# A convolution's running sum in PSUM: the taps of a centred depthwise convolution accumulated in one two-bank PSUM tile, with four PSUM banks left for the stage's products

## The chip, the core and the metric

The kernel runs on one core of a Trainium2 chip. Five engines work side by side, each through its own instructions in a fixed order: TensorE (PE in the profile, with its weight loads as PEld), VectorE (DVE), ScalarE (ACT), GpSimd (POOL) and SyncE (SP), which issues most of the DMA. ScalarE issues DMA too. The metric is the time of the whole launch on the device in microseconds (us), as a median of several runs.

## What is computed

One layer of a hybrid encoder block, over 1024 tokens and 1024 features. The part that matters here is the input projection's slice `xBC` (3072 channels), which goes through a convolution of five taps along the tokens, a bias and SiLU:

```
proj = h @ w_in[l]
q, k, v, xBC, z, dt_raw, gates = jnp.split(proj, offsets, axis=-1)
...
def depthwise_conv_centred(u, w, bias):
    pad = (w.shape[0] - 1) // 2
    out = lax.conv_general_dilated(u, w[:, None, :].astype(u.dtype), window_strides=(1,),
                                   padding=[(pad, pad)], dimension_numbers=("NWC", "WIO", "NWC"),
                                   feature_group_count=u.shape[-1])
    return out + bias

def ssd_mixer(xBC, z, dt_raw, conv_w, conv_b, A_log, dt_bias, ssd_D, ssd_norm_w):
    xBC = jax.nn.silu(depthwise_conv_centred(xBC, conv_w, conv_b))
    ...
```

After it come attention, a scan over the convolved channels, the merge of both branches and a two-layer MLP.

## The kernel before, in words

The stage that changes runs from about 415 to 716 us of the span. It makes 26 blocks of 128 channels by 1024 tokens, two blocks at a time ("a pair", 13 pairs: 12 for the convolution and one for gate channels, which is last). Matrices are float32; each operand is split into a high half (rounded, by ScalarE: CAST) and a low half (the rest, a subtraction: TENSOR_TENSOR at L154, on VectorE or on GpSimd), and a product takes three matmuls for each of four slices: high by high, high by low, low by high. So a product is 12 matmuls of 512 columns (`product`, L763 to L769), into one PSUM bank, tile `psc`.

A pair is a 2 by 2 block scheme with seven products in place of eight. `load_pair` fetches the pair's weights as two tiles, `r0` (blocks a11 and a21) and `r1` (a12 and a22), the latter with one buffer, so that the next pair's `r1` can only be fetched once this pair's last reader is done with it. GpSimd forms four sums of blocks (`ws`: sm1 to sm4). The operands `wop` of a11, a12 and a22 get their low halves from VectorE, those of sm1 to sm4 from GpSimd. The products are, in order: a11 (copied out by ScalarE as `c1`), a12 and sm2 (added by VectorE into the halves of the pair's first block, tile `pad`, called pa here), sm3 and a22 (into the second block, pb), sm1 (copied out by ScalarE as `p5`, then added by GpSimd to the right halves of pb and pa) and sm4 (added by VectorE into pa).

When a block is complete, `conv` runs: ScalarE writes tap 0 and the bias (L711), VectorE adds four more taps with four SCALAR_TENSOR_TENSOR of 128 by 1024 (L713), each reading `pad` and the accumulator `cacc` and writing `cacc`, all in SBUF, and ScalarE applies SiLU in place (L715). TensorE then transposes the result in eight pieces (`to_tokens`, tile `pst`, L730), ScalarE copies that out and stores it. `cacc` has three buffers.

The order of instructions on each engine is set at build time by a scheduler with its own estimates; the code's order is a wish. Waits are semaphores that it places. What is released in PSUM or SBUF goes to the next user of that buffer.

Of the kernel before, what the change touches and what calls it, by code (L numbers as in the profile page):

```python
# [9 lines left out]
F32 = mybir.dt.float32  # L10
F32R = mybir.dt.float32r
BF16 = mybir.dt.bfloat16
AF = mybir.ActivationFunctionType
ALU = mybir.AluOpType
# [4 lines left out]
P = 128  # L19
S = 1024  # L20
# [70 lines left out]
def block(ctx: ExitStack, tc: tile.TileContext, ia, out, upto=99, dbg=None):  # L91
    nc = tc.nc
    V, A, G, T = nc.vector, nc.scalar, nc.gpsimd, nc.tensor
# [43 lines left out]
    cwT = cp.tile([P, 120], F32, name="cwT")  # L137
    vecT = cp.tile([P, 104], F32, name="vecT")
    CB0, N1, N2, SN, BA = 0, 24, 32, 40, 56
# [117 lines left out]
    with tc.tile_pool(name="p0", bufs=1) as p0, tc.tile_pool(name="ps0", bufs=1, space=PSUM) as ps0:  # L257
# [4 lines left out]
        ps = ps0.tile([P, 512], F32, name="psv", tag="psv", bufs=2)  # L262
# [54 lines left out]
        def mod1(sl, between=None):  # L317
            g = mod_acc(p0, sl, bufs=7)
            n = 0
            try:  # L320
                while True:
                    next(g)
                    n += 1
                    if between:
                        between(n)
            except StopIteration as e:
                return e.value
# [5 lines left out]
        with tc.manual_schedule(engines={mybir.EngineType.SP, mybir.EngineType.DVE}):  # L333
# [11 lines left out]
            scale = mod1(1, first_half)  # L345
# [14 lines left out]
        ps = ps0.tile([P, 512], F32, name="psv", tag="psv", bufs=2)  # L360
# [342 lines left out]
    with tc.tile_pool(name="p2", bufs=1, reuse_waits="tile") as p2, \  # L703
            tc.tile_pool(name="ps2", bufs=1, space=PSUM, reuse_waits="tile") as ps2:

        def acc_tile():
            return p2.tile([P, S], F32, name="cacc", tag="cacc", bufs=CACC)

        def conv(i, pad):
            acc = accs.pop() if accs else acc_tile()  # L710
            A.activation(acc, pad[:, 0:S], AF.Identity, scale=cwT[:, i:i + 1], bias=vecT[:, CB0 + i:CB0 + i + 1])  # L711
            for k in range(1, 5):
                V.scalar_tensor_tensor(out=acc, in0=pad[:, k:k + S], scalar=cwT[:, 24 * k + i:24 * k + i + 1],  # L713
                                       in1=acc, op0=ALU.mult, op1=ALU.add)
            A.activation(acc, acc, AF.Silu)  # L715
            if i >= 20:
                adma(bc_d[i - 20][:, 1], acc)
                return
            if i >= 16:
                adma(bc_d[i - 16][:, 0], acc)  # L720
            late.append(lambda: to_tokens(i, acc))
# [3 lines left out]
        def to_tokens(i, y):  # L725
            st = p2.tile([P, NT, P], F32, name="cst", tag="cst", bufs=2)
            for hf in range(2):
                pt = ps2.tile([P, 512], F32, name="pst", tag="pst", bufs=2)
                for c in range(4):
                    T.transpose(pt[:, c * P:(c + 1) * P], y[:, (hf * 4 + c) * P:(hf * 4 + c + 1) * P], ident)  # L730
                A.copy(st[:, hf * 4:hf * 4 + 4], pt.rearrange("p (c n) -> p c n", c=4))
            if i >= 16:
                adma(xb_d[i - 16][:, :, 512:640], st)
            else:
                adma(xb_d[i // 4][:, :, (i % 4) * P:(i % 4 + 1) * P], st)
# [16 lines left out]
        def done(kind, i, pad):  # L752
            if kind == "conv":
                conv(i, pad)
            else:
                adma(gt_d[i], pad[:, 2:S + 2])
# [4 lines left out]
            return t  # L761

        def product(w, b):  # L763
            ps = ps2.tile([P, 512], F32, name="psc", tag="psc", bufs=6)
            for j in range(HK):
                T.matmul(ps, w[0][:, j], b[j][0], start=j == 0, stop=False)
                T.matmul(ps, w[0][:, j], b[j][1], start=False, stop=False)
                T.matmul(ps, w[1][:, j], b[j][0], start=False, stop=j == HK - 1)
            return ps  # L769
# [7 lines left out]
        H0, H1 = slice(2, 514), slice(514, 1026)  # L777
        nxt = load_pair(0)

        accs = []  # L780
        tus = [p2.tile([P, 2, 512], F32, name="u1", tag="cst", bufs=2)]
        pre = {"ws": [p2.tile([P, HK, P], F32, name="ws", tag="ws", bufs=4)],
               "c1": [p2.tile([P, 512], F32, name="c1", tag="c1", bufs=2)],
# [16 lines left out]
        for p, (kind, i0, _) in enumerate(pairs):  # L800
# [4 lines left out]
            def fifth():  # L805
                t = p2_tile("p5", [P, 512], 1)
                A.copy(t, product(w1_op(sm1, e_lo=G), H12))
                return t

            sm1 = w_sum(a21, a22, ALU.add)  # L810
            if p == LAST:
                p5 = fifth()
                for j in range(HK):
                    for q in range(2):
                        dma(H12[j][q].bitcast(F32), h12_d[q][j])
            c1 = p2_tile("c1", [P, 512], 2)
            A.copy(c1, product(w1_op(a11), H11))
            sm2 = w_sum(sm1, a11, ALU.subtract)
            tt(V, pa[:, H0], c1, product(w1_op(a12), H21), ALU.add)
            tt(V, pa[:, H1], c1, product(w1_op(sm2, e_lo=G), U2), ALU.add)  # L820
            if p == 0:
# [430 lines left out]
    with tc.tile_pool(name="p5", bufs=1, reuse_waits="tile") as p5, \  # L1252
# [41 lines left out]
        for n, (i, second) in enumerate(jobs):  # L1294
# [12 lines left out]
            for half in range(2):  # L1307
                ps = part[i][half] if i in part else ps5.tile([P, 512], F32, name="psg", tag="psg", bufs=6)
# [39 lines left out]
    with tc.tile_pool(name="p6", bufs=1, reuse_waits="tile") as p6:  # L1348
# [9 lines left out]
        def turned(hf, k):  # L1358
            ps = ps7.tile([P, 512], F32, name="pst", tag="ps1", bufs=4)
            for j in range(4):  # L1360
                T.transpose(ps[:, j * P:(j + 1) * P], x1[hf * 4 + j][:, k * P:(k + 1) * P], ident)
            return ps
# [4 lines left out]
        for t in range(NT):  # L1367
# [3 lines left out]
            for n in range(2):  # L1371
# [3 lines left out]
                ps = ps7.tile([P, 512], F32, name="pso", tag="ps2", bufs=4)  # L1375
# [12 lines left out]
            if t == 4:  # L1388
                for k in range(KT):
                    ps = turned(0, k)  # L1390
# [268 lines left out]
    with tc.tile_pool(name="p8", bufs=1, reuse_waits="tile") as p8:  # L1659
        acc = {}  # L1660
# [134 lines left out]
```

## Time and profile before

| | before |
|---|---|
| median of three runs | 2547.74 us (2547.34 to 2552.68) |
| profiled execution: its time, its span | 2555.1 us, 2553.3 us |
| TensorE busy over the span | 2422.2 us (95%) |
| VectorE, ScalarE, GpSimd busy over the span | 1779.8, 1121.7, 908.8 us |
| the pairs between 437 and 700 us: TensorE, VectorE, ScalarE, GpSimd busy | 244.83, 229.09, 127.24, 184.49 of 263.00 us |

Busy times say how full an engine is, not what holds the others up; that is read from the waits in each stretch. The profiled execution took 7.4 us more than the median of the three timed runs, and all durations here are of the profiled one.

### The profile page before, as it was taken

The page shows a single profiled execution, that of the slowest core. Times are in us where ns is not written, and L with a number is a line of the kernel's source. Part 1 is how long each engine was busy: PE and PEld are TensorE (multiplying, and loading weights), DVE is VectorE, ACT ScalarE, POOL GpSimd, SP SyncE. Part 2 cuts the span into 40 slices and gives each one's busy share as a digit, 9 for nine tenths or more (in the row PEclk, how much of TensorE's full clock was granted, in tenths as well). Part 3 has the DMA queues.
Part 4 walks back from the last instruction along what each step waited for, and adds up shares of the span by engine and source line. Part 5 has one row for each costly group of instructions (what it writes and reads, how often), then busy time and mean ns, then how long its engine had stood idle before and what let it go on. Part 6 is the DMA issues. An engine that isn't in the chain of part 4 may idle for free. (4 is left out here: it accounts for less than half of the span.)

```text
span 2553.3 us, 32339 instructions
## 1 busy us (share of the span) xinstructions
PE 2422.2 (95%) x11403; PEld 1935.0 (76%) x11403; DVE 1779.8 (70%) x2199; ACT 1121.7 (44%) x1944; POOL 908.8 (36%) x672
## 2 busy tenths in 40 slices
PE   5999999999989999999899999999898999999999
PEld 5898777777767777777667767777686888888887
DVE  5756346898866666666577787636659888667794
ACT  5455513444546666666333344343333222264430
POOL 2310107677711111110346665514107875113200
PEclk9899999999999999999999999999998999999999
DMA  7653751233541212111666675466424645464522
GB/s 262 181 164 124 231 182 62 78 96 92 165 141 58 87 54 88 55 54 50 201 194 206 190 218 164 146 197 207 152 79 140 201 151 171 177 207 132 161 84 89
DMA packets 282162, 363.38 MB, mean 142 GB/s; under 512 B 33673, under 2 KB 166513, under 8 KB 282001
## 3 DMA queue, kind: packets, MB, share of 16 engines
q1 hardware_dynamic: 209841, 285.22, 35.7%
q10 hardware_dynamic: 72160, 76.11, 8.9%
q8 instruction: 90, 1.47, 0.2%
q14 instruction: 71, 0.58, 0.1%
HBM read 248.18 MB, written 113.06 MB: 141 GB/s over the span
## 5 line engine op out<-in xcount | busy, mean ns | idle before, releaser
L891 DVE TENSOR_REDUCE nm<-pss 128x1 f32<-128x1024 f32 x128 | 156.7, 1225 | 135.1 <-PE pss L889 133.7
L380 PE MATMUL psq<-twl,hh 128*128 128x400 f32 (+1 forms) x512 | 193.1, 379 | 7.4 <-DVE twl L154 5.4
L379 PE MATMUL psq<-twh,hh 128*128 128x400 f32 (+1 forms) x512 | 192.4, 381 | 3.4 <-ACT hh L305 1.3
L381 PE MATMUL psq<-twh,hl 128*128 128x400 f32 (+1 forms) x512 | 191.7, 376 | 0.0
L893 ACT ACTIVATE pf<-pss,nm 128x1024 f32<-128x1024 f32 x128 | 142.8, 1116 | 102.1 <-PE pst L904 99.3
L154 DVE TENSOR_TENSOR pl<-pst,ph 128x512 fp32r<-128x512 f32 x256 | 167.9, 683 | 27.6 <-ACT ph L168 27.6
L904 PEld LDWEIGHTS pst<-masks,pf 128*128 128x128 f32 x1024 | 118.3, 140 | 70.1 <-issue 29.7
L168 ACT CAST ph<-pst 128x512 fp32r<-128x512 f32 x256 | 146.4, 585 | 54.2 <-PE pst L904 41.0
L904 PE MATMUL pst<-masks,pf 128*128 128x128 f32 x1024 | 157.0, 276 | 11.7 <-DVE pl L154 9.7
L713 DVE SCALAR_TENSOR_TENSOR cacc<-pad,cwT,cacc 128x1024 f32<-128x1024 f32 x96 | 163.2, 1730 | 0.4
L154 POOL TENSOR_TENSOR av<-av,rz 64x512 f32<-64x512 f32 x32 | 41.3, 1290 | 326.5 <-DMA rz<-rz 158.5
L1673 PE MATMUL p<-o,o 128*128 128x512 f32 x400 | 155.2, 389 | 0.6 <-DVE o L154 0.6
L1672 PE MATMUL p<-o,o 128*128 128x512 f32 x400 | 153.8, 390 | 1.7 <-DVE ac L154 1.4
L1674 PE MATMUL p<-o,o 128*128 128x512 f32 x400 | 153.8, 389 | 0.0
L168 ACT CAST wop<-ws 128x512 fp32r<-128x512 f32 x116 | 71.7, 621 | 103.6 <-PE pp L1332 67.5
L380 PEld LDWEIGHTS psq<-twl,hh 128*128 128x128 f32 x512 | 98.5, 192 | 19.6 <-DVE twl L154 6.5
L154 POOL TENSOR_TENSOR sl<-sl 128x512 f32<-128x512 f32 x32 | 49.6, 1553 | 178.5 <-DVE o L154 72.4
L379 PEld LDWEIGHTS psq<-twh,hh 128*128 128x128 f32 x512 | 97.8, 192 | 15.8 <-ACT qkvr L512 1.7
L381 PEld LDWEIGHTS psq<-twh,hl 128*128 128x128 f32 x512 | 97.8, 191 | 11.9 <-issue 0.9
L1106 ACT ACTIVATE e<-psd 128x512 f32<-128x512 f32 x128 | 70.8, 595 | 74.6 <-PE psd L1104 61.4
L168 ACT CAST o<-sl 128x512 fp32r<-128x512 f32 x92 | 56.9, 623 | 105.0 <-PE p L1674 88.4
L941 PE MATMUL pv<-pl,v 128*64 128x512 f32 x256 | 102.0, 419 | 0.0
(424 smaller groups left out, 7133.0 us busy)
## 6 DMA issues: line engine op xcount, KB each, us to landing
ar<-r SPq DMA_DIRECT2D x100, 256.0 KB
wada<-in_w_ada_dram SPq DMA_DIRECT2D x48, 512.0 KB
r<-in_w_mlp_dram SPq DMA_DIRECT2D x32, 512.0 KB
sl<-in_w_mlp_dram SPq DMA_DIRECT2D x64, 256.0 KB
r<-in_w_in_dram SPq DMA_DIRECT2D x26, 512.0 KB
r<-ro ACTq DMA_DIRECT2D x52, 256.0 KB
r<-as SPq DMA_DIRECT2D x48, 256.0 KB
xb<-cst ACTq DMA_DIRECT2D x20, 512.0 KB
```

The source lines that it names most:

```text
L154: e.tensor_tensor(out=o, in0=a, in1=b, op=op)
L168: (e_hi or A.copy)(hi, src)
L379: T.matmul(o, hhi[k][half][:, sl], hi[:, k % 2, :n], start=k == 0, stop=False)
L380: T.matmul(o, hhi[k][half][:, sl], lo[:, k % 2, :n], start=False, stop=False)
L381: T.matmul(o, hlo[k][half][:, sl], hi[:, k % 2, :n], start=False, stop=k == KT - 1)
L713: V.scalar_tensor_tensor(out=acc, in0=pad[:, k:k + S], scalar=cwT[:, 24 * k + i:24 * k + i + 1], in1=acc, op0=ALU.mult, op1=ALU.add)
L891: V.tensor_reduce(out=nm, in_=ps, axis=AX.X, op=ALU.max, negate=True)
L893: A.activation(pfs[u], ps, AF.Exp, bias=nm, accum_out=zall[:, u:u + 1])
L904: T.transpose(pt[:, k], pf[:, (hf * 4 + k) * P:(hf * 4 + k + 1) * P], ident)
L1672: T.matmul(ps, a[:, 0, sl], b[0], start=start, stop=False)
L1673: T.matmul(ps, a[:, 0, sl], b[1], start=False, stop=False)
L1674: T.matmul(ps, a[:, 1, sl], b[0], start=False, stop=stop)
```

## The change

The accumulator of a convolution's taps becomes a PSUM tile `tap` of 128 by 1024 float32 (two banks) with a single buffer. ScalarE writes tap 0 there, VectorE's four additions read `pad` from SBUF and `tap` from PSUM and write `tap` in PSUM, and SiLU reads `tap` and writes a `cacc` tile in SBUF. The products' tile `psc` has four banks instead of six; the transposes keep two, so that PSUM's eight banks are used before and after.

```
         def conv(i, pad):
-            acc = accs.pop() if accs else acc_tile()
-            A.activation(acc, pad[:, 0:S], AF.Identity, scale=cwT[:, i:i + 1], bias=vecT[:, CB0 + i:CB0 + i + 1])
+
+            tap = ps2.tile([P, S], F32, name="tap", tag="tap", bufs=1)
+            A.activation(tap, pad[:, 0:S], AF.Identity, scale=cwT[:, i:i + 1], bias=vecT[:, CB0 + i:CB0 + i + 1])
             for k in range(1, 5):
-                V.scalar_tensor_tensor(out=acc, in0=pad[:, k:k + S], scalar=cwT[:, 24 * k + i:24 * k + i + 1],
-                                       in1=acc, op0=ALU.mult, op1=ALU.add)
-            A.activation(acc, acc, AF.Silu)
+                V.scalar_tensor_tensor(out=tap, in0=pad[:, k:k + S], scalar=cwT[:, 24 * k + i:24 * k + i + 1],
+                                       in1=tap, op0=ALU.mult, op1=ALU.add)
+            acc = acc_tile()
+            A.activation(acc, tap, AF.Silu)
...
-            ps = ps2.tile([P, 512], F32, name="psc", tag="psc", bufs=6)
+            ps = ps2.tile([P, 512], F32, name="psc", tag="psc", bufs=4)
...
-        accs = []
```

The scheduler also orders the stage anew. Three places follow, on VectorE, ScalarE and GpSimd, each in the same pair of the steady part. Outside the stage a few dozen instructions change places with a neighbour on their engine. The tile numbers are the build's own and differ between the two builds.

VectorE before, from the sm4 addition that completes pa (`pad_4453`) on: `cacc_4605` is the accumulator of pb's convolution, `cacc_4629` that of pa's, `wop_4731` the operand of the next pair's a22, `pad_4636` the next pair's pa.

```order
L154 TENSOR_TENSOR pad_4453<-pad_4453,psc_4615 128x512
L713 SCALAR_TENSOR_TENSOR cacc_4605<-pad_4456,cwT_327,cacc_4605 128x1024 x2
L713 SCALAR_TENSOR_TENSOR cacc_4629<-pad_4453,cwT_327,cacc_4629 128x1024
L713 SCALAR_TENSOR_TENSOR cacc_4605<-pad_4456,cwT_327,cacc_4605 128x1024
L154 TENSOR_TENSOR wop_4731<-r1_4567,wop_4731 128x512
L713 SCALAR_TENSOR_TENSOR cacc_4629<-pad_4453,cwT_327,cacc_4629 128x1024
L154 TENSOR_TENSOR pad_4636<-c1_4644,psc_4667 128x512
L713 SCALAR_TENSOR_TENSOR cacc_4605<-pad_4456,cwT_327,cacc_4605 128x1024
L713 SCALAR_TENSOR_TENSOR cacc_4629<-pad_4453,cwT_327,cacc_4629 128x1024
L154 TENSOR_TENSOR pad_4636<-c1_4644,psc_4684 128x512
```

VectorE in the changed kernel, the same place: `tap_4613` is pb's sum and `tap_4638` pa's, in the same two banks one after the other; `wop_4741` is the a22 operand, `wop_4840` and `wop_4859` those of a11 and a12 of the pair after.

```order
L154 TENSOR_TENSOR pad_4461<-pad_4461,psc_4624 128x512
L714 SCALAR_TENSOR_TENSOR tap_4613<-pad_4464,cwT_327,tap_4613 128x1024 x3
L154 TENSOR_TENSOR wop_4741<-r1_4575,wop_4741 128x512
L714 SCALAR_TENSOR_TENSOR tap_4613<-pad_4464,cwT_327,tap_4613 128x1024
L154 TENSOR_TENSOR pad_4646<-c1_4654,psc_4677 128x512
L154 TENSOR_TENSOR pad_4646<-c1_4654,psc_4694 128x512
L714 SCALAR_TENSOR_TENSOR tap_4638<-pad_4461,cwT_327,tap_4638 128x1024 x2
L154 TENSOR_TENSOR pad_4649<-pad_4646,psc_4713 128x512
L154 TENSOR_TENSOR wop_4840<-r0_4758,wop_4840 128x512
L714 SCALAR_TENSOR_TENSOR tap_4638<-pad_4461,cwT_327,tap_4638 128x1024 x2
L154 TENSOR_TENSOR pad_4649<-pad_4649,psc_4744 128x512
L154 TENSOR_TENSOR wop_4859<-r1_4760,wop_4859 128x512
```

The two convolutions of a pair no longer interleave, and three taps stand ahead of the low half of a22 where four stood.

ScalarE before, over the same pair: tap 0 of pb (`cacc_4605`), tap 0 of pa (`cacc_4629`), and SiLU of pb; `cst` are copies of transposed results.

```order
L168 CAST wop_4681<-ws_4662 128x512
L711 ACTIVATE cacc_4605<-pad_4456,vecT_328,cwT_327 128x1024
L168 CAST wop_4700<-ws_4698 128x512
L731 COPY cst_4589<-pst_4590 128x512
L711 ACTIVATE cacc_4629<-pad_4453,vecT_328,cwT_327 128x1024
L731 COPY cst_4589<-pst_4596 128x512
L817 COPY c1_4644<-psc_4648 128x512
L168 CAST wop_4731<-r1_4567 128x512
L735 DMA xb_1_95<-cst_4589 1024x1x128
L168 CAST wop_4753<-ws_4642 128x512
L168 CAST wop_4795<-ws_4786 128x512
L715 ACTIVATE cacc_4605<-cacc_4605 128x1024
```

ScalarE in the changed kernel, from the copy of `p5` on: tap 0 of pb, SiLU of pb (into `cacc_4619`), then tap 0 of pa.

```order
L808 COPY p5_4577<-psc_4581 128x512
L168 CAST wop_4691<-ws_4672 128x512
L712 ACTIVATE tap_4613<-pad_4464,vecT_328,cwT_327 128x1024
L168 CAST wop_4710<-ws_4708 128x512
L733 COPY cst_4597<-pst_4598 128x512
L733 COPY cst_4597<-pst_4604 128x512
L737 DMA xb_1_95<-cst_4597 1024x1x128
L818 COPY c1_4654<-psc_4658 128x512
L168 CAST wop_4741<-r1_4575 128x512
L168 CAST wop_4763<-ws_4652 128x512
L717 ACTIVATE cacc_4619<-tap_4613 128x1024
L712 ACTIVATE tap_4638<-pad_4461,vecT_328,cwT_327 128x1024
```

Tap 0 of pa moved from ahead of pb's SiLU to behind it.

GpSimd before, over the next pair's sums: `wop_4612` is the operand of this pair's sm4, `ws_4642`, `ws_4662`, `ws_4698` and `ws_4786` the next pair's sm1 to sm4, and the last two rows add `p5` to pb and pa.

```order
L154 TENSOR_TENSOR wop_4612<-ws_4603,wop_4612 128x512
L154 TENSOR_TENSOR ws_4642<-r0_4565,r1_4567 128x512
L773 MEMSET pad_4636 128x2
L774 MEMSET pad_4636 128x2
L154 TENSOR_TENSOR ws_4662<-ws_4642,r0_4565 128x512
L154 TENSOR_TENSOR ws_4698<-r0_4565 128x512
L154 TENSOR_TENSOR ws_4786<-r1_4567,ws_4662 128x512
L773 MEMSET pad_4639 128x2
L774 MEMSET pad_4639 128x2
L154 TENSOR_TENSOR pad_4456<-pad_4456,p5_4569 128x512
L154 TENSOR_TENSOR pad_4453<-pad_4453,p5_4569 128x512
```

GpSimd in the changed kernel, over the next pair's sums: `ws_4652`, `ws_4672`, `ws_4708` and `ws_4796` are sm1 to sm4, and `wop_4621` is the operand of this pair's sm4.

```order
L154 TENSOR_TENSOR ws_4652<-r0_4573,r1_4575 128x512
L154 TENSOR_TENSOR ws_4672<-ws_4652,r0_4573 128x512
L154 TENSOR_TENSOR ws_4708<-r0_4573 128x512
L154 TENSOR_TENSOR wop_4621<-ws_4611,wop_4621 128x512
L154 TENSOR_TENSOR ws_4796<-r1_4575,ws_4672 128x512
L775 MEMSET pad_4649 128x2
L776 MEMSET pad_4649 128x2
L154 TENSOR_TENSOR pad_4464<-pad_4464,p5_4577 128x512
L154 TENSOR_TENSOR pad_4461<-pad_4461,p5_4577 128x512
```

The low half for this pair's sm4 moved from ahead of the next pair's four sums to between the third and the fourth.

## Rows read from the trace of the kernel before

**Rows 1.** The page: busy time, share of the span and instructions of each engine.

```profile
PE 2422.2 (95%) x11403; PEld 1935.0 (76%) x11403; DVE 1779.8 (70%) x2199; ACT 1121.7 (44%) x1944; POOL 908.8 (36%) x672
```

**Rows 2.** Busy time in a stretch: length, PE, PEld, DVE, ACT, POOL (instructions), clock, DMA.

```profile
437.00:700.00 263.00, 244.83 (x1135) 200.09 (x1134) 229.09 (x184) 127.24 (x192) 184.49 (x159) 0.99 0.34 105
```

**Rows 3.** Waits, 437 to 720 us: who waited for whom, total us, times, longest.

```profile
POOL ws L154 <- DMA r<-in_w_in_dram: 58.9, 11, 6.7
DVE pad L154 <- POOL pad L154: 32.2, 12, 4.6
PE psc L768 <- DVE wop L154: 18.6, 10, 2.6
PE psc L768 <- POOL wop L154: 1.6, 1, 1.6
```

**Rows 4.** Waits of the DMA queue that SyncE issues, 437 to 720 us.

```profile
SPq L748 <- DVE wop L154: 224.3, 21, 15.5
SPq L872 <- PE psc L768: 3.7, 1, 3.7
```

**Rows 5.** Timeline of TensorE (start, length, instruction, idle before and its releaser).

```profile
537.23 0.39 PE L766 MATMUL psc<-u2h,wop 128*128 128x512 f32 x1
...
542.67 0.39 PE L766 MATMUL psc<-u4h,wop 128*128 128x512 f32 x1
...
544.86 0.50 PE L768 MATMUL psc<-u4h,wop 128*128 128x512 f32 x1 [1.57 <-DVE wop L154]
...
567.60 0.50 PE L768 MATMUL psc<-u4h,wop 128*128 128x512 f32 x1 [1.57 <-DVE wop L154]
```

**Rows 6.** Timeline of VectorE.

```profile
522.02 1.27 DVE L713 SCALAR_TENSOR_TENSOR cacc<-pad,cwT,cacc 128x1024 f32<-128x1024 f32 x1
...
523.81 2.47 DVE L713 SCALAR_TENSOR_TENSOR cacc<-pad,cwT,cacc 128x1024 f32<-128x1024 f32 x2
...
535.80 8.40 DVE L713 SCALAR_TENSOR_TENSOR cacc<-pad,cwT,cacc 128x1024 f32<-128x1024 f32 x4
544.13 0.68 DVE L154 TENSOR_TENSOR wop<-r,wop 128x512 fp32r<-128x512 f32 x1
```

**Rows 7.** Timeline of GpSimd.

```profile
525.95 1.48 POOL L154 TENSOR_TENSOR ws<-r,r 128x512 f32<-128x512 f32 x1 [4.40 <-DMA r<-in_w_in_dram]
...
532.64 2.52 POOL L154 TENSOR_TENSOR pad<-pad,p 128x512 f32<-128x512 f32 x2
535.13 3.52 POOL L154 TENSOR_TENSOR wop<-ws,wop 128x512 fp32r<-128x512 f32 x2
539.60 3.52 POOL L154 TENSOR_TENSOR wop<-ws,wop 128x512 fp32r<-128x512 f32 x2 [0.95 <-ACT wop L168]
548.78 1.35 POOL L154 TENSOR_TENSOR ws<-r,r 128x512 f32<-128x512 f32 x1 [5.65 <-DMA r<-in_w_in_dram]
```

**Rows 8.** Instructions by tile: count, duration ns min/median/max, first and last start us.

```profile
L713 DVE SCALAR_TENSOR_TENSOR cacc<-pad,cwT,cacc x96: 1272/1704/2324, 442.8 to 710.7; 128x1024 f32<-128x1024 f32 x96
L154 DVE TENSOR_TENSOR pad<-pad,psc x39: 673/687/691, 438.0 to 715.5; 128x512 f32<-128x512 f32 x39
L154 POOL TENSOR_TENSOR pad<-pad,p x26: 1085/1092/1473, 440.0 to 716.4; 128x512 f32<-128x512 f32 x26
L154 DVE TENSOR_TENSOR wop<-r,wop x36: 677/1636/1785, 437.4 to 707.7; 128x512 fp32r<-128x512 f32 x36
L154 POOL TENSOR_TENSOR ws<-r,ws x11: 1278/1287/2290, 459.9 to 692.9; 128x512 f32<-128x512 f32 x11
```

**Rows 9.** Groups of instructions by line, ScalarE in the stage and VectorE's reduction of attention.

```profile
L711 ACT ACTIVATE cacc<-pad,vecT,cwT 128x1024 f32<-128x1024 f32 x24 | 29.9, 1247 | 21.2 <-POOL pad L154 21.1
L715 ACT ACTIVATE cacc<-cacc 128x1024 f32<-128x1024 f32 x24 | 25.5, 1063 | 104.4 <-DVE cacc L713 104.4
L807 ACT COPY p<-psc 128x512 f32<-128x512 f32 x13 | 7.6, 586 | 7.5 <-ACT cst L731 4.6 <-PE psc L768 2.9
L891 DVE TENSOR_REDUCE nm<-pss 128x1 f32<-128x1024 f32 x128 | 156.7, 1225 | 135.1 <-PE pss L889 133.7
```

## The prediction

> **What bounds the kernel now.** The page comes first: TensorE is busy 95% of the span [rows 1]. That is an average over stages, so I go to the stage that changes. Its busy times show TensorE at work for 244.83 of 263.00 us [rows 2]: 18 us of it idle. The waits of the stage say on whom it waits: 18.6 us, in ten waits, for VectorE's low half of an operand, and 1.6 us once for GpSimd's [rows 3]. TensorE's timeline gives the rhythm: two of these waits end 22.74 us apart (544.86 and 567.60), each after 1.57 us idle [rows 5]. So a pair takes 22.74 us, and 21.17 of it is TensorE at work.
>
> Why is VectorE late, each time by much the same? Followed through the timelines of GpSimd and VectorE, one loop closes over a pair. GpSimd starts a pair's first sum at 525.95, when a weight tile has landed, and is done with its four sums at 532.64 and with the two `p5` additions at 535.16 [rows 7]. VectorE completes pa and starts the first tap at 535.80; four taps later, at 544.13, comes the low half of a22, done at 544.81 [rows 6], where TensorE goes on [rows 5]. That low half also frees the tile `r1`: SyncE's loads wait 224.3 us in all for VectorE's `wop` rows [rows 4]. The next tile lands 3.97 us later and GpSimd starts again at 548.78. The steps, start to start, are 6.69 + 3.16 + 8.33 + 0.68 + 3.97 = 22.83 us, the pair's length. So this loop, through fetch, GpSimd and VectorE, sets the pace, and TensorE waits 1.6 us a pair for it.
>
> The largest step is the four taps, 2.1 us each. The reader should compare: while GpSimd waits for its tile, up to 525.95, the same instruction takes 1.27 us, and two in a row 2.47, or 1.24 each [rows 6, 7]; while GpSimd works (535.13 to 543.12) four take 8.40. Over the stage it runs from 1272 to 2324 ns; low halves, which also read two SBUF operands, from 677 to 1785; GpSimd's `ws` sums from 1278 to 2290. But the additions with one operand in PSUM stay within 673 to 691 in all 39 cases [rows 8], in a stage in which GpSimd is busy 70% of the time [rows 2]. So VectorE with two SBUF operands and GpSimd slow each other; with one it goes undisturbed. [...]
>
> **The change, part by part.** *The taps' price, s.* The 96 taps now read one SBUF operand and one in PSUM, and write PSUM. Bounds: from below 1.24 us, the undisturbed one above; VectorE's reduction of 1024 columns out of two PSUM banks takes 1.225 [rows 9], so reading PSUM costs nothing visible. VectorE writing PSUM, or reading and writing one bank in one instruction, has no row. From above 2.47, twice the undisturbed one, should a bank's read and write take turns; disturbed taps reach 2.32 today. The rows nearest in kind are the 1.225 and the additions from PSUM, so I take 1.30, 5% over the undisturbed tap for the write, and keep 1.24 to 2.47 for the range.
>
> *GpSimd* no longer meets the taps: a sum or a low half falls to 1.28, a `p5` addition to 1.09 [rows 8].
>
> *The fetch loop, redone.* In the new order three taps, not four, stand ahead of a22's low half, but GpSimd has one more operation ahead of the `p5` additions: 5 x 1.28 + 2 x 1.09 + 0.69 + 3s + 0.68 + 3.97 = 13.9 + 3s, or 17.8 us at 1.30, against TensorE's 21.17. If low half and sums still disturb each other it grows by about 2; that still fits.
>
> *The single tile is a new wait.* Tap 0 of the second convolution now stands behind the first one's SiLU, and the next pair's behind the second's. Over a pair the tile's own loop is eight taps, two taps 0 at 1.25, two SiLU at 1.06, on ScalarE a copy of `p5` and one cast like it at 0.59 [rows 9], on VectorE one addition of 0.69 and two low halves between the taps (0.68 to 1.64 each), and some eight hand-offs of 0.05, as from the low half's end at 544.81 to TensorE's start at 544.86. That is 8s + 8.2 to 10.2; I take 8s + 9.2, the middle. At 1.30 it gives 19.6, below 21.17: covered by TensorE's work. The cover ends at s = 1.50; at s = 1.69 the loop reaches today's 22.74. What queues behind a late SiLU on ScalarE are casts for the next products, and TensorE waits for those.
>
> *Four banks for the products.* A product's bank is needed again after three other products instead of five, that is 36 matmuls at 5.44/24 = 0.227 us (24 of them lie between 537.23 and 542.67 [rows 5]): 8.2 us. The addition for sm4 is the one that starts late today, by up to 4.6 us behind GpSimd [rows 3], and it gets earlier. Cost nothing, hidden under those 8.2 us; without them a product would wait out the rest of the 4.6.
>
> *The rest.* ScalarE is busy 127 of 263 us [rows 2]; tap 0 into PSUM and SiLU out of it may shift by some hundredths, under that slack. The `cacc` tiles are held for less time. No DMA is added or taken away; the fetch of `r1` comes earlier. The swaps outside the stage I cost at nothing.
>
> *The sum.* Both loops fall under TensorE's own 21.17, so TensorE's waits go: 18.6 + 1.6 = 20.2 us. A tap cheaper than 1.30 adds nothing, since TensorE then sets the pace. The profiled execution took 2555.1, 7.4 over the median: 2534.9 for its like, and from the median 2547.74 - 20.2 = **2527.5 us**.
>
> [...] By the rows an operand in PSUM is free: 1.225 for the reduction. [...]
>
> **The rivals.** *Slower: the taps cost 1.69 us or more in PSUM.* Then the tile's loop sets the pace. For it: no row shows VectorE writing PSUM, and every tap reads what the one before it has just written there. Against it: the reduction's 1.225. There are 11 periods between the 12 convolution pairs, so at 2.0 it is (25.2 - 22.74) x 11 = +27, 2575 us; at 2.47, (29.0 - 22.74) x 11 = +69, 2616.
>
> *Half the gain: s between 1.50 and 1.69,* or the loop's fixed part at its upper end. At 1.60 a pair takes 22.0 and the gain is 0.74 x 11 = 8: 2540 us, between 2531 and 2546.
>
> *The change doesn't do what it says: the taps stay disturbed,* at today's median 1.70 [rows 8]. For it: they still read `pad` and their scalar from SBUF. Against it: the 39 additions. The loop then takes 22.8, with slow low halves 23.8: 0 to +12, 2548 to 2560.
>
> *Given back later.* The stage ends 20 us sooner but what follows does not. For it: attention's first loads. Against it: they wait for TensorE's products of this stage [rows 4] and so move along. 2540 to 2550.
>
> **How the numbers follow.** Forecast 0.66, with its own range 2521 to 2532 (down if idle time that is not in the waits goes too); half 0.13; slower taps 0.11; disturbed taps 0.04; given back 0.06. The range to 2547 takes in the forecast, the half and most of the given back, 0.83; the tail of dear taps stays out. A measurement here tells about 0.2%, 5 us, from no change. Faster: 0.66, nearly all of the half and some of the given back, 0.78. Slower: the dear taps and most of the disturbed ones, 0.14. Same: 0.08.
>
> **What would show it.** Right: taps of 1.25 to 1.40 with little spread; GpSimd's sums near 1.28; TensorE's waits for VectorE's `wop` all but gone; pairs 21.2 us apart; GpSimd's waits for the weight tile longer than today's 58.9 us in all [rows 3], since the fetch loop has slack. Wrong: taps of 1.5 or more, SiLU or tap 0 as the last thing that transposes and products wait for, TensorE waiting for a bank behind VectorE's additions.

## The result, and the profile after

The changed kernel takes 2521.32 us (median of 4 runs, 2520.33 to 2523.71) against 2548.84 for the kernel before in the same comparison (4 runs, 2547.34 to 2552.68): ratio 0.9891, 95% interval 0.9874 to 0.9908. That is 27.5 us less, where 20.2 were forecast; 2521.3 lies at the lower end of the range. A second comparison (e_again below) gave 0.987 (0.9854 to 0.9885).

The page of the changed kernel, against [rows 1]:

```profile
PE 2418.8 (96%) x11403; PEld 1937.3 (77%) x11403; DVE 1724.4 (68%) x2199; ACT 1125.7 (45%) x1944; POOL 867.8 (34%) x672
```

TensorE's work is what it was; VectorE has 55 us less and GpSimd 41 us less, with the same number of instructions. So instructions became shorter. The stretch of [rows 2], and under it the part of it that now belongs to the stage (columns as there):

```profile
437.00:700.00 263.00, 261.36 (x1228) 217.20 (x1227) 189.44 (x198) 141.20 (x203) 156.87 (x164) 1.00 0.43 133
...
437.00:688.00 251.00, 251.00 (x1185) 209.29 (x1184) 186.40 (x195) 136.45 (x197) 154.00 (x163) 1.00 0.41 121
```

TensorE is at work in all of the 251 us. The waits of 437 to 700 us, against [rows 3]:

```profile
POOL wop L154 <- ACT wop L168: 47.9, 13, 4.5
ACT wop L168 <- PE psc L770: 43.6, 30, 2.1
DVE pad L154 <- POOL pad L154: 33.0, 11, 3.5
DVE pad L154 <- PE psc L770: 25.3, 17, 3.3
...
POOL pad L154 <- ACT p L808: 20.5, 10, 2.4
ACT cacc L717 <- DVE tap L714: 11.0, 14, 2.0
...
POOL ws L154 <- DMA r<-in_w_in_dram: 2.7, 2, 1.6
...
ACT tap L712 <- ACT cacc L717: 0.8, 2, 0.4
```

TensorE's lines are gone: nothing in this stretch of the stage makes it wait. The others now wait for it: ScalarE and VectorE for products (`psc`), GpSimd for ScalarE's casts and for `p5`, which wait for products in their turn. The single tile held tap 0 up for 0.8 us in all. VectorE's timeline over one pair, against [rows 6]:

```profile
524.25 0.69 DVE L154 TENSOR_TENSOR pad<-pad,psc 128x512 f32<-128x512 f32 x1 [3.38 <-POOL pad L154]
524.86 3.93 DVE L714 SCALAR_TENSOR_TENSOR tap<-pad,cwT,tap 128x1024 f32<-128x1024 f32 x3
528.89 0.69 DVE L154 TENSOR_TENSOR wop<-r,wop 128x512 fp32r<-128x512 f32 x1
...
545.10 0.69 DVE L154 TENSOR_TENSOR pad<-pad,psc 128x512 f32<-128x512 f32 x1 [3.43 <-POOL pad L154]
```

A pair takes 20.85 us (524.25 to 545.10), not 22.74. Last, the instructions by tile, against [rows 8, 9]:

```profile
L714 DVE SCALAR_TENSOR_TENSOR tap<-pad,cwT,tap x96: 1275/1284/1291, 442.7 to 684.2; 128x1024 f32<-128x1024 f32 x96
L154 DVE TENSOR_TENSOR wop<-r,wop x36: 677/692/1799, 437.3 to 676.4; 128x512 fp32r<-128x512 f32 x36
L712 ACT ACTIVATE tap<-pad,vecT,cwT x24: 1206/1209/1212, 441.0 to 678.0; 128x1024 f32<-128x1024 f32 x24
L717 ACT ACTIVATE cacc<-tap x24: 1019/1027/1032, 449.2 to 685.5; 128x1024 f32<-128x1024 f32 x24
L154 POOL TENSOR_TENSOR wop<-ws,wop x52: 1267/1292/1756, 420.9 to 678.2; 128x512 fp32r<-128x512 f32 x52
L888 PE MATMUL pss<-k,q x256: 387/395/501, 695.8 to 1189.7; 128*128 128x512 f32 x128
```

All 96 taps lie within 16 ns; before they spread from 1272 to 2324. VectorE's low halves, which still read two SBUF operands, have a median of 0.69 and still a maximum of 1.80. GpSimd became faster too: the median of its 52 low halves was 1.78 before and is 1.29 now.

**Where the 28 us came from.** The last line gives a clean measure: attention's first score product starts at 695.8, before at 724.2 (below). Counted from the first product of the stage, 416.0 and 415.9, the stage takes 279.8 us and took 308.3: 28.5 less. Attention is as long as before (494 us between the first and last start of that line in both), so nothing is given back. What is left of the program differs by 3 us between the two profiled executions, and over all those shown here it varies between 1326.7 and 1336.2 us from run to run and program to program, though its source is the same; so below the stage is the sharper measure, and a median can carry some 5 us of the rest. The stage has a scatter of its own: the changed kernel's two traces give 279.8 and 281.3, so a difference of 1.5 us or less says nothing.

The waits were 20.2 us; the stage gave 28.5. Three pieces of the kernel before that [rows 5] didn't show fill most of the gap. Its timeline of TensorE at one of the longer waits:

```profile
496.33 0.39 PE L767 MATMUL psc<-u4l,wop 128*128 128x512 f32 x1
499.36 0.50 PE L768 MATMUL psc<-u4h,wop 128*128 128x512 f32 x1 [2.64 <-DVE wop L154]
499.69 0.40 PE L766 MATMUL psc<-u4h,wop 128*128 128x512 f32 x1
...
500.62 0.59 PE L767 MATMUL psc<-u4l,wop 128*128 128x512 f32 x1
501.01 0.63 PE L768 MATMUL psc<-u4h,wop 128*128 128x512 f32 x1
...
504.00 0.43 PE L766 MATMUL psc<-hh,wop 128*128 128x512 f32 x1
504.26 0.39 PE L767 MATMUL psc<-hl,wop 128*128 128x512 f32 x1
```

Two windows of the same trace (columns of [rows 2]; the last three are granted clock, DMA share and GB/s):

```profile
500.60:504.00 3.40, 3.40 (x10) 2.63 (x9) 3.40 (x4) 1.57 (x2) 0.88 (x1) 0.51 0.48 146
...
708.80:712.20 3.40, 3.40 (x10) 2.63 (x9) 3.40 (x5) 0.27 (x2) 0.00 (x0) 0.51 1.02 324
```

And the same line of attention as above, by tile:

```profile
L887 PE MATMUL pss<-k,q x256: 387/395/501, 724.2 to 1218.1; 128*128 128x512 f32 x128
```

First, idle time is counted from the end of a matmul's 0.39 us, but in a run they start 0.227 apart. The wait of 2.64 lies between two starts 3.03 apart, and the next start comes 0.33 later: 3.36 for two steps that take 0.45, so it cost 2.91, 0.27 more than its idle time. Over the eleven waits that is 3.0 us. Second, behind two of them the clock fell to a lower level (granted 0.51, where it was 1.00 from 499.4 to 500.6): nine steps from 500.62 to 504.26 in 3.64 us in place of 2.04, so 1.6 us, and as much at 708.8. Third, the first gate product behind the pairs waited 0.9 us for VectorE's last addition (`pad`), which came late. 20.2 + 3.0 + 3.2 + 0.9 = 27.3 of the 28.5; for the last 1.2 no row was found, and it lies within the scatter.

### The profile page after: what moved, and what is told of

Same layout as the page of the kernel before. It is cut to its first block, busy times and chain, and to the rows that moved or that the text cites. A ratio compares the mean times of both kernels' runs of the same rounds, so it can differ in the third digit from the quotient of the medians.

```text
span 2521.9 us, 32355 instructions
## 1 busy us (share of the span) xinstructions
PE 2418.8 (96%) x11403; PEld 1937.3 (77%) x11403; DVE 1724.4 (68%) x2199; ACT 1125.7 (45%) x1944; POOL 867.8 (34%) x672
## 5 line engine op out<-in xcount | busy, mean ns | idle before, releaser
L714 DVE SCALAR_TENSOR_TENSOR tap<-pad,cwT,tap 128x1024 f32<-128x1024 f32 x96 | 123.4, 1285 | 5.1 <-ACT tap L712 3.7
L381 PEld LDWEIGHTS psq<-twh,hl 128*128 128x128 f32 x512 | 98.3, 192 | 12.7 <-issue 0.9
```

What stands on the lines that cost most here:

```text
L381: T.matmul(o, hlo[k][half][:, sl], hi[:, k % 2, :n], start=False, stop=k == KT - 1)
L714: V.scalar_tensor_tensor(out=tap, in0=pad[:, k:k + S], scalar=cwT[:, 24 * k + i:24 * k + i + 1], in1=tap, op0=ALU.mult, op1=ALU.add)
```

## The experiments

Medians in us, ratio to the kernel before run beside each group with its 95% interval (its medians there are 2551.53 to 2553.53, so a ratio is not the median over 2548.84), and the stage from the first product's start to attention's first score product in the profiled execution:

```
                  median    ratio                     stage
before            2548.84   1                         308.3
changed           2521.32   0.9891 (0.9874-0.9908)    279.8
e_again           2519.92   0.9870 (0.9854-0.9885)    281.3
e_banks4          2548.55   0.9987 (0.9977-0.9996)    304.8
e_single_sbuf     2561.70   1.0036 (1.0023-1.0050)    320.9
e_last_sbuf       2522.05   0.9896 (0.9881-0.9911)    279.9
e_gp_off          2516.14   one run                   273.4
e_extra1          2524.51   0.9895 (0.9878-0.9911)    279.8
e_extra2          2537.27   0.9946 (0.9932-0.9960)    292.5
e_extra2_last     2527.92   0.9900 (0.9885-0.9914)    285.7
e_psc3            2528.78   0.9903 (0.9889-0.9917)    284.1
e_open4           2526.47   0.9898 (0.9884-0.9912)    280.6
e_open2           2520.38   0.9868 (0.9852-0.9884)    280.7
e_open_sb         2511.53   0.9838 (0.9825-0.9852)    274.7
```

**The theory** is the prediction's: a tap with two SBUF operands and GpSimd's instructions slow each other, and the place in PSUM ends that. **The rival**: the gain comes from what came with it, fewer product banks or the scheduler's new order (three taps, not four, ahead of a22's low half).

**e_banks4**: the kernel before, with the banks alone changed.

```
-            ps = ps2.tile([P, 512], F32, name="psc", tag="psc", bufs=6)
+            ps = ps2.tile([P, 512], F32, name="psc", tag="psc", bufs=4)
```

> The kernel before with one edit: four banks for the products in place of six; the running sum stays in SBUF. Theory (the sum's place in PSUM makes the gain, the banks cost nothing): within 0.2% of the kernel before, ratio 0.998 to 1.002; taps still from 1.27 to 2.3 us with a median near 1.7; TensorE still waits some 20 us in the stage for VectorE's low half. Rival (four banks, by holding products back or by the other order of instructions that comes with them, make the gain or a part of it): ratio 0.990 to 0.995. Third case (the banks do cost, and the gain hid it): ratio above 1.002.

Ratio 0.9987: the first case. Its taps by tile:

```profile
L713 DVE SCALAR_TENSOR_TENSOR cacc<-pad,cwT,cacc x96: 1271/1486/2320, 437.9 to 702.9; 128x1024 f32<-128x1024 f32 x96
```

They spread as before, but their median is 1.49 and not near 1.7, and TensorE waits 16.7 us in twelve waits for VectorE's low half, not some 20. The stage is 3.5 us shorter. So the four banks, or the order of instructions that the scheduler makes for them, may give up to that much; which of the two was not followed further.

**e_single_sbuf**: the changed kernel, the tile back in SBUF.

```
-            tap = ps2.tile([P, S], F32, name="tap", tag="tap", bufs=1)
+            tap = p2.tile([P, S], F32, name="tap", tag="tap", bufs=1)
```

> The changed kernel with its one accumulator tile put back into SBUF; still one tile, four banks, and nearly the same order on every engine. Theory (place in PSUM): the taps have two SBUF operands again and are disturbed, 1.6 to 2.1 us each; the tile's own loop 8s + 9.2 is then 22.0 to 26.0 us against TensorE's 20.85, so the time is 2534 to 2578, ratio to the kernel before 0.995 to 1.012, and TensorE waits again. Rival (the order does it: the low half of a22 behind three taps instead of four, the earlier fetch): time near the changed kernel's, ratio 0.988 to 0.991, TensorE without waits.

The order of GpSimd's instructions and of the loads is that of the changed kernel, and nearly so on the others; the place in PSUM alone makes 41 us of stage (320.9 against 279.8). The rival falls. Of the 41 us, 26 are longer waits of TensorE; most of the rest is the lower clock behind some of them (granted 0.83 from 500 to 520 us, 0.87 from 540 to 560). Its waits from 437 to 735 us:

```profile
POOL pad L775 <- DVE tap L714: 22.5, 10, 3.7
...
PE psc L770 <- POOL wop L154: 20.0, 7, 4.0
```

One pair in its timeline of VectorE:

```profile
585.19 5.25 DVE L714 SCALAR_TENSOR_TENSOR tap<-pad,cwT,tap 128x1024 f32<-128x1024 f32 x3
590.36 1.78 DVE L154 TENSOR_TENSOR wop<-r,wop 128x512 fp32r<-128x512 f32 x1
...
600.89 4.48 DVE L714 SCALAR_TENSOR_TENSOR tap<-pad,cwT,tap 128x1024 f32<-128x1024 f32 x2
```

Two taps take 4.48 here, 2.60 or 2.61 in the changed kernel. The mean of the 96 is 1.827; the tile's loop would by the prediction's 8s + 9.2 be 23.8, and SiLU starts at 496.83 and, four pairs on, at 593.37: 24.1. The lateness reaches TensorE by a way that the prediction didn't have: a late tap holds its `pad` tile, GpSimd's memset of that tile waits (22.5 us in all), and behind the memset stand the low halves for which TensorE waits (20.0).

**e_gp_off**: the kernel before, GpSimd's sums and low halves left out.

```
         def w_sum(a, b, op):
-            t = p2_tile("ws", [P, HK, P], 4)
-            tt(G, t, a, b, op)
-            return t
+            return a
...
-        tt(e_lo or V, lo, src, hi.bitcast(F32), ALU.subtract)
+        if e_lo is not SKIP:
+            tt(e_lo or V, lo, src, hi.bitcast(F32), ALU.subtract)
...
-        return hi, lo
+        return hi, hi if e_lo is SKIP else lo
...
-                A.copy(t, product(w1_op(sm1, e_lo=G), H12))
+                A.copy(t, product(w1_op(sm1, e_lo=SKIP), H12))
```

(the same for the products of sm2, sm3 and sm4.)

> The kernel before, sums in SBUF, with GpSimd's weight sums and low halves of the stage left out: a product takes an operand that is there already, and its high half twice, so that GpSimd does only the two additions of p5 and some memsets; TensorE's work is the same. Theory (VectorE with two SBUF operands and GpSimd slow each other): the taps fall to 1.24 to 1.30 us with little spread, the low halves on VectorE to 0.68, a pair takes TensorE's 20.9 us, time about 2515 to 2525. Rival (taps are slow for a reason of VectorE's own, ScalarE's or the DMA's traffic): the median stays at 1.6 us or more and taps above 2 remain, whatever the time does.

Its taps by tile:

```profile
L715 DVE SCALAR_TENSOR_TENSOR cacc<-pad,cwT,cacc x96: 1271/1279/2108, 440.5 to 674.1; 128x1024 f32<-128x1024 f32 x96
```

With GpSimd quiet, taps that read two SBUF operands take 1.28 us, a median 0.43 below [rows 8]; a 2.11 is left, and GpSimd still has the `p5` additions. So GpSimd's work is what slows them: with e_single_sbuf, cause and cure are both shown.

**e_last_sbuf**: the last tap writes SBUF.

```
+            acc = acc_tile()
             for k in range(1, 5):
-                V.scalar_tensor_tensor(out=tap, in0=pad[:, k:k + S], scalar=cwT[:, 24 * k + i:24 * k + i + 1],
+                V.scalar_tensor_tensor(out=acc if k == 4 else tap, in0=pad[:, k:k + S], scalar=cwT[:, 24 * k + i:24 * k + i + 1],
                                        in1=tap, op0=ALU.mult, op1=ALU.add)
-            acc = acc_tile()
-            A.activation(acc, tap, AF.Silu)
+            A.activation(acc, acc, AF.Silu)
```

> The changed kernel, but the last of the four taps writes its result to the SBUF tile that SiLU then works on in place; the PSUM tile is free one SiLU earlier. Theory (one PSUM operand is what keeps a tap undisturbed, and TensorE sets the pace): the last tap takes 1.24 to 1.30 us as the other three do, with little spread; the time is that of the changed kernel, ratio to the kernel before 0.988 to 0.991. Rival (it is the write into PSUM that keeps GpSimd away): the last taps spread up to 1.6 or more. Second rival (the single tile is what limits the changed kernel still): one SiLU and two hand-offs less in its loop, 1.1 us a convolution or up to 2 us a pair, ratio 0.980 to 0.984.

Its last taps by tile:

```profile
L715 DVE SCALAR_TENSOR_TENSOR cacc<-pad,cwT,tap x24: 1271/1276/1282, 446.3 to 682.2; 128x1024 f32<-128x1024 f32 x24
```

No spread: the operand read from PSUM, not the write into it, is what keeps a tap undisturbed. The time is the changed kernel's, so the single tile doesn't set its pace.

**e_extra1 and e_extra2**: how much room has the tile's loop? One tap more in one convolution of a pair, and in both.

```
-            for k in range(1, 5):
+            for k in (1, 2, 3, 4, 4)[:4 + i % 2]:
```

```
-            for k in range(1, 5):
+            for k in (1, 2, 3, 4, 4):
```

> The changed kernel with a fifth tap (the last one a second time) in one of a pair's two convolutions, so the output has a tap too many there. It asks how much room the single tile's own loop has. Theory (the loop is 8s + 9.2, now 19.4 us at the 1.28 measured, under TensorE's 20.85): one tap more makes it 20.7, still covered: the time stays that of the changed kernel, ratio to the kernel before 0.988 to 0.991, TensorE without waits in the stage's middle. Rival (the loop's fixed part is at its upper end, 10.2, or the single tile is already the limit): 21.7 us a pair, 0.85 x 11 = 9 us more and a few for restarts, ratio 0.992 to 0.996.

> The same with the fifth tap in both convolutions of a pair. Theory: the loop is 19.4 + 2.6 = 22.0 us against 20.85, so TensorE waits 1.15 us a pair, 13 us over 11 periods, and 3 to 9 more since each wait also costs a drained pipeline and sometimes a stretch at the lower clock; 2534 to 2543, ratio to the kernel before 0.993 to 0.999. SiLU or tap 0 comes to stand in the chain that TensorE waits for. Rival (the loop's fixed part is at its lower end, 8.2, or the scheduler's other order shortens it): 21.0 us a pair, ratio 0.988 to 0.991.

Both came out as the theory had them: the first stage is 279.8 us, unchanged; the second 292.5, 12.7 more. But the way was another. The second one's timeline of ScalarE, with SiLU of one pair and of the tenth after it, and the end:

```profile
469.16 1.03 ACT L717 ACTIVATE cacc<-tap 128x1024 f32<-128x1024 f32 x1 [1.25 <-DVE tap L714]
...
690.57 1.02 ACT L717 ACTIVATE cacc<-tap 128x1024 f32<-128x1024 f32 x1 [4.87 <-DVE tap L714]
...
699.87 1.02 ACT L717 ACTIVATE cacc<-tap 128x1024 f32<-128x1024 f32 x1 [6.66 <-DVE tap L714]
701.29 0.58 ACT L854 COPY ost<-psg 128x512 f32<-128x512 f32 x1 [0.40 <-ACT cacc L717]
```

Its timeline of TensorE there:

```profile
701.93 0.80 PE L206 MATMUL psg<-hh,whi 128*128 128x512 f32 x1 [11.92 <-ACT ost L854]
```

SiLU comes 22.14 us apart from pair to pair ((690.57 - 469.16) / 10; 22.0 was expected), but TensorE does not wait 1.15 us in each pair, as the theory had it. It goes on at its own pace and starts the last matmul of the pairs at 684.2. The taps run ever later behind it, and TensorE pays once, 11.9 us, when the first copy of the next stage (`ost`, of a gate product) stands behind the last SiLU on ScalarE.

**e_extra2_last**: five taps, but the fifth writes SBUF, so SiLU leaves the tile's loop.

```
-            for k in (1, 2, 3, 4, 4):
-                V.scalar_tensor_tensor(out=tap, in0=pad[:, k:k + S], scalar=cwT[:, 24 * k + i:24 * k + i + 1],
+            acc = acc_tile()
+            for n, k in enumerate((1, 2, 3, 4, 4)):
+                V.scalar_tensor_tensor(out=acc if n == 4 else tap, in0=pad[:, k:k + S], scalar=cwT[:, 24 * k + i:24 * k + i + 1],
                                        in1=tap, op0=ALU.mult, op1=ALU.add)
-            acc = acc_tile()
-            A.activation(acc, tap, AF.Silu)
+            A.activation(acc, acc, AF.Silu)
```

> The changed kernel with five taps in both convolutions, as in the run that lost 13 us or so, but the fifth tap writes to the SBUF tile in which SiLU works, so SiLU is out of the PSUM tile's loop. Theory (that loss was the loop's 22.24 us a pair against 20.85): the loop is 2 x 1.08 shorter, 20.1 us, and covered again: ratio to the kernel before 0.988 to 0.992. Rival (the loss comes from VectorE's 2.6 us more work a pair, or from the other order of its instructions, not from the tile): ratio to the kernel before 0.993 to 0.997 as with five taps.

Ratio 0.9900, inside the theory's range: SiLU now starts 20.86 us apart, pair by pair (560.60, 581.45, 602.31, and so on to 664.87), so the loop is covered, with VectorE's 2.6 us of extra work still in each pair. About half of the loss stays (stage 285.7): at the end TensorE still waits 3.9 us for the last SiLU.

**e_psc3**: three banks for the products, against **e_again**, the changed kernel on the same chip.

```
-            ps = ps2.tile([P, 512], F32, name="psc", tag="psc", bufs=4)
+            ps = ps2.tile([P, 512], F32, name="psc", tag="psc", bufs=3)
```

> The changed kernel with three banks for the products in place of four, one bank left empty. A product's bank is then needed again after 24 matmuls, 5.4 us, in place of 36, 8.2. Theory (the additions that empty a bank come at most 4.6 us late, mostly 3): still covered, ratio to the changed kernel 0.999 to 1.002. Rival (the banks are close to their limit at four): TensorE waits for an addition in each pair, 1 to 3 us, 11 to 33 us in all, ratio to it 1.004 to 1.013.

> The changed kernel itself once more, as the measure for the three others on the same chip: ratio to the kernel before 0.988 to 0.991.

e_again came out at 0.9870, just under its range. Between the two, 2528.78 to 2519.92 is 1.0035, outside the theory's range and a little under the rival's. The trace is neither: from 437 to 688 us TensorE waits for nothing, so 5.4 us of cover is enough for the pairs. One wait at the opening grew, 6.3 us for VectorE's addition out of a bank (4.0 for another cause in e_again), since this addition stood behind the opening's sums on VectorE. The stage is only 2.8 us longer than e_again's; the other 6 lie in the program's unchanged rest, without a cause that was found.

**The opening.** e_gp_off's stage was 6.4 us shorter than the changed kernel's at the same pace of pairs. The changed kernel's timeline of VectorE in the opening:

```profile
423.96 3.47 DVE L154 TENSOR_TENSOR hl<-u,hh 128x512 fp32r<-128x512 f32 x2
427.35 0.68 DVE L154 TENSOR_TENSOR u<-hh,hh 128x512 f32<-128x512 f32 x1
427.95 1.77 DVE L154 TENSOR_TENSOR u<-hl,hl 128x512 f32<-128x512 f32 x1
...
433.04 2.35 DVE L154 TENSOR_TENSOR u<-u 128x512 f32<-128x512 f32 x2
```

Its timeline of TensorE beside it:

```profile
432.20 0.39 PE L770 MATMUL psc<-hh,wop 128*128 128x512 f32 x1
435.49 0.80 PE L768 MATMUL psc<-hh,wop 128*128 128x512 f32 x1 [2.90 <-ACT hh L168]
436.22 0.80 PE L769 MATMUL psc<-hl,wop 128*128 128x512 f32 x1
```

Four operands are summed there on VectorE, again with two SBUF operands beside GpSimd. **e_open4** puts all four sums into PSUM tiles, **e_open2** the last two:

```
-                tu = tus.pop() if tus else p2.tile([P, 2, 512], F32, name="u1", tag="cst", bufs=2)
-                t, u = tu[:, 0], tu[:, 1]
+                t = ps2.tile([P, 512], F32, name="u1p", tag="pst", bufs=2)
                 tt(V, t, H12[j][0].bitcast(F32), H11[j][0].bitcast(F32), ALU.subtract)
-                tt(V, u, H12[j][1].bitcast(F32), H11[j][1].bitcast(F32), ALU.subtract)
-                tt(V, t, t, u, ALU.add)
+                tt(V, t, t, H12[j][1].bitcast(F32), ALU.add)
+                tt(V, t, t, H11[j][1].bitcast(F32), ALU.subtract)
                 split(*H12[j], t)
```

> The changed kernel, and the same idea at the stage's opening: the four operands that VectorE sums there (two differences added) get their running sum in a PSUM tile, so two of each sum's three additions, and the low half, read one SBUF operand and not two. In the changed kernel four of these instructions took 1.70 to 1.78 us beside GpSimd's sums (0.68 without), TensorE waited 2.9 us for them at 432.6 and 0.7 at 423.4, and ran at the lower clock for the next nine matmuls. Theory (the same contention): the opening's waits go, 3 to 6.5 us less than the changed kernel, 2515 to 2519, ratio to the kernel before 0.985 to 0.989. Rival (these waits are set by GpSimd's sums or the PSUM tiles that come free late, not by VectorE): no change or slower, ratio 0.989 to 0.992.

> The same for only the last two of the four operands, the ones beside which GpSimd is at work; the first two keep their SBUF tiles and are begun before the stage. Theory: most of the gain of the other, or all of it if PSUM tiles come free too late for the first two: ratio to the kernel before 0.985 to 0.989. Rival as there: 0.989 to 0.992.

Neither shortened the stage (280.6, 280.7); the better ratio of e_open2 lies outside it, so it is not put down to the edit. TensorE waited 4.2 us for the same operand in e_open2, and in e_open4 2.0 us for an addition and 1.0 for a low half, both VectorE's: VectorE's first use of the second PSUM tile waited 3.4 and 3.1 us for a copy of the stage before, that is for the bank. The idea was tried where its tile isn't free, so these two say nothing against the theory. The rows above show a second cause: the third sum begins no earlier than 427.35 because its tile is the first one's, held until that one's low half is done. **e_open_sb** gives it a tile that lies idle:

```
-                tu = tus.pop() if tus else p2.tile([P, 2, 512], F32, name="u1", tag="cst", bufs=2)
+                if j < 2:
+                    tu = tus.pop() if tus else p2.tile([P, 2, 512], F32, name="u1", tag="cst", bufs=2)
+                else:
+                    tu = p2.tile([P, 2, 512], F32, name="u1", tag="cacc", bufs=CACC)
```

> The changed kernel; at the stage's opening the third and fourth of the four sums no longer wait for the two tiles of the first and second (their additions stood behind these tiles' low halves, from 427.35 on), but use two accumulator tiles that are idle until the first SiLU. Theory (the opening's waits of 2.9 and 0.7 us and the stretch at the lower clock behind them come from these late sums; the kernel without GpSimd's sums had none of them and ended the stage 6.6 us earlier): 3 to 6.6 us less than the changed kernel, ratio to it 0.9974 to 0.9988. Rival (GpSimd's sums or the products' own order set these waits): ratio to it 0.999 to 1.002.

Its timeline of VectorE in the opening:

```profile
414.86 1.78 DVE L154 TENSOR_TENSOR u<-hh,hh 128x512 f32<-128x512 f32 x1
416.57 1.78 DVE L154 TENSOR_TENSOR u<-hl,hl 128x512 f32<-128x512 f32 x1
...
425.68 1.17 DVE L154 TENSOR_TENSOR u<-u 128x512 f32<-128x512 f32 x1
```

The third sum begins at 414.86, and of TensorE's waits in the opening and the pairs one of 0.4 us is left. The stage is 6.6 us shorter than e_again's (5.1 than that of the changed kernel's first trace), the upper end of what the theory had, and the kernel the fastest of this study: 2511.53 us (2510.51 to 2513.42), 0.9967 of e_again beside it, whose runs go from 2516.32 up. That ratio is better than the theory's range; the part beyond the stage's 6.6 us lies in the unchanged rest. The instructions are still slow, 1.78 each, so the opening's waits went without any of them becoming faster. That does not clear contention: in e_gp_off the third sum still stands behind the first two low halves (it begins at 423.27), but these instructions take 0.68 each, and TensorE waits for none of them. Either cure is enough.

## Why the prediction was right, point by point

- **What bounded the kernel** (the loop through fetch, GpSimd and VectorE): borne out by other runs. In e_banks4 its steps have other lengths, and the pair has the same: VectorE's two steps are

```profile
528.99 7.35 DVE L713 SCALAR_TENSOR_TENSOR cacc<-pad,cwT,cacc 128x1024 f32<-128x1024 f32 x4
536.26 1.75 DVE L154 TENSOR_TENSOR wop<-r,wop 128x512 fp32r<-128x512 f32 x1
```

and with GpSimd's sums from 519.17, its `p5` additions from 526.21 and its next sum at 541.76 they make 7.04 + 2.78 + 7.27 + 1.75 + 3.75 = 22.59 us, where TensorE's waits lie 22.7 apart. e_gp_off took GpSimd's sums out of the loop and reached 20.85 us a pair. In the changed kernel GpSimd's steps became shorter along with the taps, and the order changed as well, so its own gain can't be divided among the steps.
- **The taps' price**: 1.30 was taken, 1.284 is the duration, all undisturbed. The prediction's reading that an operand in PSUM is free holds: e_gp_off's taps, with both operands in SBUF, have a median of 1.279. What it left out is that taps of one sum wait for each other. Two in a row, first in the changed kernel, then undisturbed in SBUF in e_single_sbuf, where one tile also lets only taps of one sum follow each other:

```profile
533.80 2.61 DVE L714 SCALAR_TENSOR_TENSOR tap<-pad,cwT,tap 128x1024 f32<-128x1024 f32 x2
...
713.77 2.61 DVE L714 SCALAR_TENSOR_TENSOR tap<-pad,cwT,tap 128x1024 f32<-128x1024 f32 x2
```

That is the same time in both memories. The two of [rows 6] that take 2.47 belong to two sums, as the order in the section on the change shows. Start to start it is 1.31 to 1.32 us within one sum, in PSUM (40 steps) as in SBUF (10 undisturbed steps of e_single_sbuf), and 1.20 where the next tap belongs to another sum. So the single tile, which ends the interleaving, costs 0.12 us a step, and the place in PSUM nothing that these runs show. As the prediction said, a tap's price changes no total while TensorE sets the pace.
- **The fetch loop**: under TensorE's pace, as forecast. But GpSimd's wait for the weight tile did not grow past the 58.9 us of [rows 3]; it fell to 2.7. This sign was read wrongly: the slack shows up where the chain from TensorE ends last, as 47.9 us of waits for ScalarE's casts.
- **The tile's own loop**: 8s + 9.2, 19.6 forecast. From e_extra2's 22.14 with ten taps of 1.285 the fixed part is 9.3. The limits that the prediction drew from it hold: one tap more a pair is covered, two are not. Not so the way the cost arrives: not as a wait for casts in each pair, but through held `pad` tiles (e_single_sbuf), or as a debt that TensorE pays at the end (e_extra2).
- **Four banks cost nothing**: right; e_banks4 loses nothing, and three banks still hold between the pairs.
- **The sum** is the term that was mis-sized: 20.2 us of waits, 28.5 of stage. A wait's idle time was taken for its cost. The 21.17 of "TensorE at work" in a pair had in it the 0.27 us that a wait cost beyond its idle time (20.85 measured), and the two stretches at the lower clock weren't counted at all. "Given back later" fell: attention is as long as it was.

## What to carry to other kernels

When VectorE's instruction with two SBUF operands has a wide spread of durations and GpSimd is busy beside it, try one operand in PSUM: here 1.70 became 1.28, and the spread went. With a single buffer the instructions of one sum then follow each other, 0.12 us later each than those of two sums in turn. Price a wait of TensorE by the distance between the starts on either side, and look at the granted clock behind it; the idle column alone gave 20 of 28 us. Where an instruction is late, look first whether it waits for a tile that another use still holds: that was worth 6.6 us in the opening, with the instructions as slow as before.

## What was unexpected of the hardware

ScalarE is a little faster with PSUM on one side: tap 0 takes 1.209 us into PSUM and 1.247 into SBUF [rows 9], SiLU 1.027 out of PSUM and 1.063 out of SBUF: 38 and 36 ns less.

Behind a wait TensorE's clock did not always fall: after those of 1.57 us of [rows 5], and after one of 2.62 at 614.2, the matmuls go on 0.23 apart; after those of 2.64 and 2.04 nine steps were at the lower level (granted 0.51). Which waits bring it on can't be told from so few.
